# Four batches side by side on the partitions, and a softmax that reduces with transposing VectorE instructions

## Chip, core, metric

One core of a Trainium2 chip. The metric is the device time of one execution in microseconds, the median of several.

## The reference

```python
B, N, D = 8, 4096, 512                       # x and y: float32, 64 MB each
gram = np.matmul(x, y.transpose(0, 2, 1))
diag = np.diagonal(gram, axis1=1, axis2=2)   # only the row-by-row dot products matter
diag = diag - diag.max(axis=-1, keepdims=True)
exp = np.exp(diag)
return exp / exp.sum(axis=-1, keepdims=True) # a softmax over the 4096 rows of each batch
```

## The kernel before

Each batch is spread over all 128 partitions, 32 neighbouring rows (64 KB) on each. There are eight steps of 16 MB. In six of them VectorE multiplies and then sums whole tiles. In the last two it makes one dot product per instruction, and the very last step comes in pieces of 16, 8, 4, 2, 1 and 1 rows, so that little is left to do when the last row lands. A softmax needs the maximum and the sum over all 128 partitions; GpSimd (POOL in the profile) makes both.

```python
xv = x.rearrange("b (p r) d -> b p r d", p=P)         # 64 KB from partition to partition
...                                                   # yv, ov alike; cut
def load_y(b, r0, n):
    nc.sync.dma_start(out=ys[:, r0 : r0 + n, :], in_=yv[b, :, r0 : r0 + n, :])
...                                                   # multiply, sum, dot_row: cut
def group_out(name, b0, n, ssum):                     # batches 0 to 4, then 5 and 6
    ...                                               # reciprocal, scale: cut
    nc.scalar.dma_start(out=ov[:, b0 : b0 + n, :], in_=res[:, b0 : b0 + n, :])

def last_softmax(b):                                  # the tail
    db, rb = diag[:, b, :], res[:, b, :]
    ...
    nc.vector.tensor_reduce(out=mxp, in_=db, axis=X, op=Alu.max)
    nc.gpsimd.partition_all_reduce(out_ap=mx, in_ap=mxp, channels=P, reduce_op=bass_isa.ReduceOp.max)
    nc.vector.tensor_single_scalar(out=nmx, in_=mx, scalar=-1.0, op=Alu.mult)
    nc.scalar.activation(out=rb, in_=db, func=Act.Exp, bias=nmx, scale=1.0, accum_out=sump)
    nc.gpsimd.partition_all_reduce(out_ap=ssum, in_ap=sump, channels=P, reduce_op=bass_isa.ReduceOp.add)
    nc.vector.reciprocal(out=rc, in_=ssum)
    nc.vector.tensor_single_scalar(out=rb, in_=rb, scalar=rc, op=Alu.mult)
    nc.scalar.dma_start(out=ov[:, b, :], in_=rb)
```

Of the kernel before, what the change touches and what calls it, by code (L numbers as in the profile page):

```python
# [1 line left out]

# [5 lines left out]


@with_exitstack
def kernel(
    ctx: ExitStack,
    tc: tile.TileContext,
    x: bass.AP,
    y: bass.AP,
    out: bass.AP,
):
    nc = tc.nc
    ctx.enter_context(tc.manual_schedule())  # L20
    f32 = mybir.dt.float32
    Alu = mybir.AluOpType
    Act = mybir.ActivationFunctionType
    X = mybir.AxisListType.X
    B, N, D = x.shape
    P = nc.NUM_PARTITIONS
    R = N // P
    wide = B - 2


    xv = x.rearrange("b (p r) d -> b p r d", p=P)
    yv = y.rearrange("b (p r) d -> b p r d", p=P)
    ov = out.rearrange("b (p r) -> p b r", p=P)

    big = ctx.enter_context(tc.tile_pool(name="big", bufs=1))
    small = ctx.enter_context(tc.tile_pool(name="small", bufs=1))


    xs = [big.tile([P, R, D], f32, name=f"xs{i}") for i in range(2)]
    ys = big.tile([P, R, D], f32, name="ys")  # L40

    K = 6
    side = big.tile([P, K, D], f32, name="side")
    diag = small.tile([P, B, R], f32, name="diag")
    res = small.tile([P, B, R], f32, name="res")

    def column(name, n):
        return small.tile([P, n], f32, name=name)

    def load_x(b, r0, n):  # L50
        nc.sync.dma_start(out=xs[b % 2][:, r0 : r0 + n, :], in_=xv[b, :, r0 : r0 + n, :])  # L51

    def load_y(b, r0, n):
        nc.sync.dma_start(out=ys[:, r0 : r0 + n, :], in_=yv[b, :, r0 : r0 + n, :])  # L54

    def dots_wide(b, r0, n, yt):
        xt = xs[b % 2][:, r0 : r0 + n, :]
        nc.vector.tensor_tensor(out=xt, in0=xt, in1=yt, op=Alu.mult)  # L58

    def sums_wide(b):  # L60
        nc.vector.tensor_reduce(out=diag[:, b, :], in_=xs[b % 2], axis=X, op=Alu.add)  # L61

    def dot_row(b, r):
        xt = xs[b % 2]
        nc.vector.scalar_tensor_tensor(  # L65
            out=xt[:, r, :],
            in0=xt[:, r, :],
            scalar=1.0,
            in1=ys[:, r, :],
            op0=Alu.mult,  # L70
            op1=Alu.mult,
            accum_out=diag[:, b, r : r + 1],
        )

    def group_exp(name, b0, n):

        mxp, mx, nmx, sump, ssum = (column(name + s, n) for s in ("mxp", "mx", "nmx", "sump", "ssum"))
        nc.vector.tensor_reduce(out=mxp, in_=diag[:, b0 : b0 + n, :], axis=X, op=Alu.max)  # L78
        nc.gpsimd.partition_all_reduce(out_ap=mx, in_ap=mxp, channels=P, reduce_op=bass_isa.ReduceOp.max)  # L79
        nc.scalar.mul(nmx, mx, -1.0)  # L80
        for i in range(n):
            nc.scalar.activation(  # L82
                out=res[:, b0 + i, :], in_=diag[:, b0 + i, :], func=Act.Exp,
                bias=nmx[:, i : i + 1], scale=1.0, accum_out=sump[:, i : i + 1],
            )
        nc.gpsimd.partition_all_reduce(out_ap=ssum, in_ap=sump, channels=P, reduce_op=bass_isa.ReduceOp.add)  # L86
        return ssum

    def group_out(name, b0, n, ssum):
        rc = column(name + "rc", n)  # L90
        nc.vector.reciprocal(out=rc, in_=ssum)  # L91
        for i in range(n):
            rb = res[:, b0 + i, :]
            nc.scalar.activation(out=rb, in_=rb, func=Act.Copy, scale=rc[:, i : i + 1])  # L94
        nc.scalar.dma_start(out=ov[:, b0 : b0 + n, :], in_=res[:, b0 : b0 + n, :])

    def last_softmax(b):
        db, rb = diag[:, b, :], res[:, b, :]
        mxp, mx, nmx, sump, ssum, rc = (column("l" + s, 1) for s in ("mxp", "mx", "nmx", "sump", "ssum", "rc"))
        nc.vector.tensor_reduce(out=mxp, in_=db, axis=X, op=Alu.max)  # L100
        nc.gpsimd.partition_all_reduce(out_ap=mx, in_ap=mxp, channels=P, reduce_op=bass_isa.ReduceOp.max)  # L101
        nc.vector.tensor_single_scalar(out=nmx, in_=mx, scalar=-1.0, op=Alu.mult)  # L102
        nc.scalar.activation(out=rb, in_=db, func=Act.Exp, bias=nmx, scale=1.0, accum_out=sump)  # L103
        nc.gpsimd.partition_all_reduce(out_ap=ssum, in_ap=sump, channels=P, reduce_op=bass_isa.ReduceOp.add)  # L104
        nc.vector.reciprocal(out=rc, in_=ssum)  # L105
        nc.vector.tensor_single_scalar(out=rb, in_=rb, scalar=rc, op=Alu.mult)  # L106
        nc.scalar.dma_start(out=ov[:, b, :], in_=rb)

    for b in range(wide):
        load_x(b, 0, R)  # L110
        load_y(b, 0, R)
        nc.scalar.activation(out=side, in_=ys[:, R - K :, :], func=Act.Copy)  # L112
        dots_wide(b, 0, R - K, ys[:, : R - K, :])
        dots_wide(b, R - K, K, side)
        if b == wide - 1:
            group_out("a", 0, wide - 1, first)
        sums_wide(b)
        if b == wide - 2:
            first = group_exp("a", 0, wide - 1)

    b = B - 2
    load_x(b, 0, R)
    for r0 in (0, R // 2):
        load_y(b, r0, R // 2)
        for r in range(r0, r0 + R // 2):
            dot_row(b, r)

    b = B - 1
    r0 = 0
    for n in (16, 8, 4, 2, 1, 1):  # L130
        load_x(b, r0, n)
        load_y(b, r0, n)
        for r in range(r0, r0 + n):
            if r == 2:
                second = group_exp("b", B - 3, 2)
            if r == 10:
                group_out("b", B - 3, 2, second)
            dot_row(b, r)
        r0 += n
    last_softmax(b)  # L140


# [1 line left out]
_INS = ['x', 'y']  # L144
_OUTS = [((8, 4096), 'float32')]


# [23 lines left out]
```

## Time and profile before

| | before |
|---|---|
| time, median of the first 3 runs | 322.36 us |
| span of the profiled run | 320.3 us |
| loads, first packet to last (packet records) | 1.7 to 314.3 us |
| last landing of y to start of the last dot product | 314.76, 314.85 us |
| start of the last dot product to issue of the last store | 3.08 us |
| issue of the last store to the end | 2.4 us |

The page of the kernel before. The rows of busy tenths have 40 slices of 8 us; "q1" is the load queue and "q10" the store queue, with packets, MB and their share of the 16 DMA engines' time.

```profile
span 320.3 us, 310 instructions
...
DVE 247.8 (77%) x154; ACT 22.7 (7%) x32; POOL 3.3 (1%) x10
...
DMA  9999999999999999999999999999999999999991
GB/s 393 393 393 524 393 393 516 401 393 483 434 393 450 466 393 409 507 393 393 524 393 393 507 409 393 466 450 393 442 475 393 393 456 411 447 419 420 419 411 46
...
q1 hardware_dynamic: 3888, 134.22, 97.3%
q10 hardware_dynamic: 1072, 0.13, 0.3%
...
L58 DVE TENSOR_TENSOR xs<-xs,ys 128x13312 f32<-128x13312 f32 x6 | 84.2, 14025 | 62.6 <-DMA ys<-in_y_dram 62.6
```

The DMA engines are at nine tenths in every slice but the last, and the load queue alone fills 97.3% of them. VectorE (DVE) is busy 77% and waits 62.6 us for y. So this is a kernel at the limit of its loads: nothing that VectorE, ScalarE or POOL saves in mid-stream can shorten it. Time can be gained in two places only: in the load stream itself, and in the tail after the last landing.

The tail, from the timeline (start, duration, engine, line of the kernel and instruction; in brackets how long the engine had been idle, and for whom; ACT is ScalarE, and ACTq its queue, which issues the stores):

```profile
314.85 0.69 DVE L65 SCALAR_TENSOR_TENSOR xs<-xs,ys 128x512 f32<-128x512 f32 x1 [0.57 <-DMA ys<-in_y_dram]
...
315.58 0.19 DVE L100 TENSOR_REDUCE lmxp<-diag 128x1 f32<-128x32 f32 x1
315.87 0.37 POOL L101 PARTITION_ALL_REDUCE lmx<-lmxp  x1 [16.88 <-DVE lmxp L100]
316.26 0.15 DVE L102 TENSOR_SCALAR lnmx<-lmx 128x1 f32<-128x1 f32 x1 [0.49 <-POOL lmx L101]
316.45 0.32 ACT L103 ACTIVATE res<-diag,lnmx 128x32 f32<-128x32 f32 x1 [14.57 <-DVE lnmx L102]
316.68 0.19 ACT L103 ACTIVATION_READ_ACCUMULATOR res<-diag,lnmx 128x1 f32 x1
316.96 0.40 POOL L104 PARTITION_ALL_REDUCE lssum<-lsump  x1 [0.72 <-ACT res L103]
317.39 0.16 DVE L105 RECIPROCAL lrc<-lssum 128x1 f32<-128x1 f32 x1 [0.97 <-POOL lssum L104]
317.66 0.24 DVE L106 TENSOR_SCALAR res<-res,lrc 128x32 f32<-128x32 f32 x1
317.93 0.35 ACTq L107 DMA_DIRECT2D out_dram<-res  x1
```

The two POOL reductions take 0.37 and 0.40 us (spans on POOL are rough in this profile), and each costs hand-overs from VectorE or ScalarE to POOL and back, that is, waits of one engine for the other's signal. The store is issued 3.08 us after the last dot product starts.

Two pieces of the chain of waits (start, duration, what):

```profile
301.92 8.14 DMA out_dram<-res
...
310.12 4.64 DMA ys<-in_y_dram
```

The chain says that the last load of y, issued at 310.12, had waited 8.14 us for the 32 KB store of batches 5 and 6. The two share a completion count (the counter by which the kernel learns that a transfer has landed), so one must end before the other is issued.

### The profile page before, as it was taken

To read this page: it belongs to the slowest core of one execution; us is meant where nothing else is said; L and a number is where in the kernel's file an instruction comes from. 1 tells how busy PE (TensorE), PEld (TensorE's weight loads), DVE (VectorE), ACT (ScalarE), POOL (GpSimd) and SP (SyncE) were. 2 spreads that over 40 slices of the span, in tenths; PEclk is the share of its full clock that TensorE was granted. 3 is DMA by queue.
4 is the path that set the end of the run, shared out by engine and by line. 5 is a ranking of instruction groups with operands and counts; after the bars stand their busy time and mean duration, and the time that the engine had idled before them with its cause. 6 is when DMAs were issued, how large, how long until landed. Compare 5 with 4: busy or idle time off the path is not lost.

```text
span 320.3 us, 310 instructions
## 1 busy us (share of the span) xinstructions
DVE 247.8 (77%) x154; ACT 22.7 (7%) x32; POOL 3.3 (1%) x10
## 2 busy tenths in 40 slices
DVE  0000079995999949999499994999959999993994
ACT  1000030000300002000200003000050100000100
POOL 0000000000000000000000000000000000000100
DMA  9999999999999999999999999999999999999991
GB/s 393 393 393 524 393 393 516 401 393 483 434 393 450 466 393 409 507 393 393 524 393 393 507 409 393 466 450 393 442 475 393 393 456 411 447 419 420 419 411 46
DMA packets 4961, 134.36 MB, mean 419 GB/s; under 512 B 1504, under 2 KB 1504, under 8 KB 2272
## 3 DMA queue, kind: packets, MB, share of 16 engines
q1 hardware_dynamic: 3888, 134.22, 97.3%
q10 hardware_dynamic: 1072, 0.13, 0.3%
q14 instruction: 1, 0.01, 0.0%
HBM read 134.22 MB, written 0.13 MB: 419 GB/s over the span
## 4 chain that ended last, share of the span: by engine, by line
DMA 60%; DVE 36%; issue 2%; SPq 0%; POOLq 0%; ACT 0%; POOL 0%; DVEq 0%; ACTq 0%
DMA ys<-in_y_dram 57%; DVE xs L58 27%; DVE xs L65 5%; DVE diag L61 4%; DMA out_dram<-res 3%; POOLq L166 0%; ACT res L94 0%; SPq L51 0%; POOL lmx L101 0%; DVE res L106 0%; DVE lmxp L100 0%; DVE lrc L105 0%; DVE bmxp L78 0%; SPq L54 0%; DVEq L58 0%
## 5 line engine op out<-in xcount | busy, mean ns | idle before, releaser
L58 DVE TENSOR_TENSOR xs<-xs,ys 128x13312 f32<-128x13312 f32 x6 | 84.2, 14025 | 62.6 <-DMA ys<-in_y_dram 62.6
L61 DVE TENSOR_REDUCE diag<-xs 128x32 f32<-128x16384 f32 x6 | 103.3, 17220 | 0.2
L65 DVE SCALAR_TENSOR_TENSOR xs<-xs,ys 128x512 f32<-128x512 f32 x64 | 39.6, 689 | 5.7 <-DMA ys<-in_y_dram 5.6
L112 ACT ACTIVATE side<-ys 128x3072 f32<-128x3072 f32 x6 | 16.6, 2763 | 185.3 <-DMA ys<-in_y_dram 185.3
L58 DVE TENSOR_TENSOR xs<-xs,side 128x3072 f32<-128x3072 f32 x6 | 20.1, 3352 | 0.0
L65 DVE DVE_READ_ACCUMULATOR xs<-xs,ys 128x1 f32 x64 | 5.4, 84 | 0.0
L80 ACT ACTIVATE bnmx<-bmx 128x2 f32<-128x2 f32 x1 | 0.2, 203 | 42.8 <-POOL bmx L79 42.8
L79 POOL PARTITION_ALL_REDUCE amx<-amxp x1 | 0.4, 386 | 231.5 <-DVE amxp L78 231.5
L80 ACT ACTIVATE anmx<-amx 128x5 f32<-128x5 f32 x1 | 0.2, 208 | 32.7 <-POOL amx L79 32.7
L94 ACT ACTIVATE res<-res,arc 128x32 f32<-128x32 f32 x5 | 1.2, 310 | 14.8 <-DVE arc L91 14.8
L82 ACT ACTIVATE res<-diag,anmx 128x32 f32<-128x32 f32 x5 | 1.5, 309 | 0.0
L79 POOL PARTITION_ALL_REDUCE bmx<-bmxp x1 | 0.7, 736 | 61.7 <-DVE bmxp L78 61.7
L103 ACT ACTIVATE res<-diag,lnmx 128x32 f32<-128x32 f32 x1 | 0.3, 321 | 14.6 <-DVE lnmx L102 14.6
L112 ACT ACT_TABLE_LOAD x1 | 1.3, 1283 | 0.7 <-PEq L155 0.7
L82 ACT ACTIVATION_READ_ACCUMULATOR res<-diag,anmx 128x1 f32 x5 | 0.9, 188 | 0.0
L105 DVE RECIPROCAL lrc<-lssum 128x1 f32<-128x1 f32 x1 | 0.2, 164 | 1.0 <-POOL lssum L104 1.0
L86 POOL PARTITION_ALL_REDUCE bssum<-bsump x1 | 0.8, 797 | 1.1 <-ACT res L82 1.1
L94 ACT ACTIVATE res<-res,brc 128x32 f32<-128x32 f32 x2 | 0.5, 312 | 3.2 <-DVE brc L91 3.2
L82 ACT ACTIVATE res<-diag,bnmx 128x32 f32<-128x32 f32 x2 | 0.6, 314 | 0.0
L101 POOL PARTITION_ALL_REDUCE lmx<-lmxp x1 | 0.4, 367 | 16.9 <-DVE lmxp L100 16.9
L102 DVE TENSOR_SCALAR lnmx<-lmx 128x1 f32<-128x1 f32 x1 | 0.2, 153 | 0.5 <-POOL lmx L101 0.5
L86 POOL PARTITION_ALL_REDUCE assum<-asump x1 | 0.5, 459 | 2.0 <-ACT res L82 2.0
(13 smaller groups left out, 2.7 us busy)
## 6 DMA issues: line engine op xcount, KB each, us to landing
ys<-in_y_dram SPq DMA_DIRECT2D x3, 4096.0 KB, 15.0
xs<-in_x_dram SPq DMA_DIRECT2D x1, 4096.0 KB, 14.7
xs<-in_x_dram SPq DMA_DIRECT2D x1, 2048.0 KB, 19.2
ys<-in_y_dram SPq DMA_DIRECT2D x1, 2048.0 KB, 19.6
xs<-in_x_dram SPq DMA_DIRECT2D x1, 1024.0 KB, 8.0
ys<-in_y_dram SPq DMA_DIRECT2D x1, 1024.0 KB, 10.2
xs<-in_x_dram SPq DMA_DIRECT2D x1, 512.0 KB, 11.0
ys<-in_y_dram SPq DMA_DIRECT2D x1, 512.0 KB, 11.7
```

The costliest lines, as they stand in the source:

```text
L58: nc.vector.tensor_tensor(out=xt, in0=xt, in1=yt, op=Alu.mult)
L61: nc.vector.tensor_reduce(out=diag[:, b, :], in_=xs[b % 2], axis=X, op=Alu.add)
L65: nc.vector.scalar_tensor_tensor(out=xt[:, r, :], in0=xt[:, r, :], scalar=1.0, in1=ys[:, r, :], op0=Alu.mult, op1=Alu.mult, accum_out=diag ...
L79: nc.gpsimd.partition_all_reduce(out_ap=mx, in_ap=mxp, channels=P, reduce_op=bass_isa.ReduceOp.max)
L80: nc.scalar.mul(nmx, mx, -1.0)
L82: nc.scalar.activation(out=res[:, b0 + i, :], in_=diag[:, b0 + i, :], func=Act.Exp, bias=nmx[:, i : i + 1], scale=1.0, accum_out=sump[:, i ...
L86: nc.gpsimd.partition_all_reduce(out_ap=ssum, in_ap=sump, channels=P, reduce_op=bass_isa.ReduceOp.add)
L94: nc.scalar.activation(out=rb, in_=rb, func=Act.Copy, scale=rc[:, i : i + 1])
L101: nc.gpsimd.partition_all_reduce(out_ap=mx, in_ap=mxp, channels=P, reduce_op=bass_isa.ReduceOp.max)
L102: nc.vector.tensor_single_scalar(out=nmx, in_=mx, scalar=-1.0, op=Alu.mult)
L103: nc.scalar.activation(out=rb, in_=db, func=Act.Exp, bias=nmx, scale=1.0, accum_out=sump)
L112: nc.scalar.activation(out=side, in_=ys[:, R - K :, :], func=Act.Copy)
```

## The change

The intent: four batches lie side by side, each on 32 partitions, with 128 rows (256 KB) per partition. A maximum or a sum then has to cross only 32 partitions, which a VectorE reduction that transposes 32x32 blocks can do, without POOL. The Trainium skill, "VectorE: DVE Perf Modes", section "The three transpose paths", describes VectorE's transpose as a grid of independently transposed 32x32 blocks, hence one batch per 32 partitions. Batches 0 to 3 take four steps and batches 4 to 7 four more. The steps move the same bytes in the same pieces as before, but neighbouring partitions now read addresses 256 KB apart instead of 64 KB. The maximum over the early columns is taken before the last rows land, and the stores become 256 packets of 512 B instead of 1024 of 128 B.

```diff
-    xv = x.rearrange("b (p r) d -> b p r d", p=P)
-    yv = y.rearrange("b (p r) d -> b p r d", p=P)
-    ov = out.rearrange("b (p r) -> p b r", p=P)
+    xv = x.rearrange("(s b) (j c) d -> s (b j) c d", b=Q, j=G)      # Q = 4, G = 32
+    yv = y.rearrange("(s b) (j c) d -> s (b j) c d", b=Q, j=G)
+    ov = out.rearrange("(s b) (j c) -> s (b j) c", b=Q, j=G)
 ...                                                # loads and products: same sizes, cut
+    def over_quadrant(name, column, op, negate=False):
+        got = small.tile([P, 1], f32, name=name)
+        nc.vector.tensor_reduce(
+            out=got, in_=column.to_broadcast([P, G]), axis=X, op=op, negate=negate, apply_transpose=True
+        )
+        return got
 ...                                                # group_exp, group_out, last_softmax go
+    def exps(i, d):
+        mxp = small.tile([P, 1], f32, name=f"mxp{i}")
+        largest(mxp, d)
+        nmx = over_quadrant(f"nmx{i}", mxp, Alu.max, negate=True)
+        sump = small.tile([P, 1], f32, name=f"sump{i}")
+        nc.scalar.activation(out=res[i], in_=diag[i][:, :C], func=Act.Exp, bias=nmx, scale=1.0, accum_out=sump)
+        return sump
+    def store(i, sump, n):
+        total = over_quadrant(f"sum{i}", sump, Alu.add)
+        rc = small.tile([P, 1], f32, name=f"rc{i}")
+        nc.vector.reciprocal(out=rc, in_=total)
+        nc.vector.tensor_single_scalar(out=res[i], in_=res[i], scalar=rc, op=Alu.mult)
+        for p in range(0, P, n):
+            nc.scalar.dma_start(out=ov[i, p : p + n, :], in_=res[i][p : p + n, :])
 ...                                                # steps 0 to 6: cut
     for n in (16, 8, 4, 2, 1, 1):
         load_x(t, r0, n)
         load_y(t, r0, n)
+        if r0 == 0:
+            largest(diag[1][:, C : C + 1], diag[1][:, : C - R])
+        if r0 == R - 2:
+            largest(diag[1][:, C + 1 :], diag[1][:, C - R : C - 2])
         dots(t, r0, n)
         r0 += n
+    store(1, exps(1, diag[1][:, C - 2 :]), P)
```

More of the change, by code (lines that the diff above doesn't have):

```diff
@@ L26 @@
     P = nc.NUM_PARTITIONS
-    R = N // P
-    wide = B - 2
-    xv = x.rearrange("b (p r) d -> b p r d", p=P)
-    yv = y.rearrange("b (p r) d -> b p r d", p=P)
-    ov = out.rearrange("b (p r) -> p b r", p=P)
+    G = 32
+    Q = P // G
+    C = N // G
+    R = 32
+    H = R // 2
+    K = 6
+    S = B // Q * (C // R)
+    xv = x.rearrange("(s b) (j c) d -> s (b j) c d", b=Q, j=G)
+    yv = y.rearrange("(s b) (j c) d -> s (b j) c d", b=Q, j=G)
+    ov = out.rearrange("(s b) (j c) -> s (b j) c", b=Q, j=G)
     big = ctx.enter_context(tc.tile_pool(name="big", bufs=1))
@@ L40 @@
     ys = big.tile([P, R, D], f32, name="ys")
-    K = 6
     side = big.tile([P, K, D], f32, name="side")
-    diag = small.tile([P, B, R], f32, name="diag")
-    res = small.tile([P, B, R], f32, name="res")
-    def column(name, n):
-        return small.tile([P, n], f32, name=name)
-    def load_x(b, r0, n):
-        nc.sync.dma_start(out=xs[b % 2][:, r0 : r0 + n, :], in_=xv[b, :, r0 : r0 + n, :])
-    def load_y(b, r0, n):
-        nc.sync.dma_start(out=ys[:, r0 : r0 + n, :], in_=yv[b, :, r0 : r0 + n, :])
@@ L56, in dots_wide @@
-    def dots_wide(b, r0, n, yt):
-        xt = xs[b % 2][:, r0 : r0 + n, :]
-        nc.vector.tensor_tensor(out=xt, in0=xt, in1=yt, op=Alu.mult)
-    def sums_wide(b):
-        nc.vector.tensor_reduce(out=diag[:, b, :], in_=xs[b % 2], axis=X, op=Alu.add)
-    def dot_row(b, r):
-        xt = xs[b % 2]
-        nc.vector.scalar_tensor_tensor(
-            out=xt[:, r, :],
-            in0=xt[:, r, :],
-            scalar=1.0,
-            in1=ys[:, r, :],
-            op0=Alu.mult,
-            op1=Alu.mult,
-            accum_out=diag[:, b, r : r + 1],
-        )
@@ L75, in group_exp @@
-    def group_exp(name, b0, n):
-        mxp, mx, nmx, sump, ssum = (column(name + s, n) for s in ("mxp", "mx", "nmx", "sump", "ssum"))
-        nc.vector.tensor_reduce(out=mxp, in_=diag[:, b0 : b0 + n, :], axis=X, op=Alu.max)
-        nc.gpsimd.partition_all_reduce(out_ap=mx, in_ap=mxp, channels=P, reduce_op=bass_isa.ReduceOp.max)
-        nc.scalar.mul(nmx, mx, -1.0)
-        for i in range(n):
-            nc.scalar.activation(
-                out=res[:, b0 + i, :], in_=diag[:, b0 + i, :], func=Act.Exp,
-                bias=nmx[:, i : i + 1], scale=1.0, accum_out=sump[:, i : i + 1],
-            )
-        nc.gpsimd.partition_all_reduce(out_ap=ssum, in_ap=sump, channels=P, reduce_op=bass_isa.ReduceOp.add)
-        return ssum
@@ L89, in group_out @@
-    def group_out(name, b0, n, ssum):
-        rc = column(name + "rc", n)
-        nc.vector.reciprocal(out=rc, in_=ssum)
-        for i in range(n):
-            rb = res[:, b0 + i, :]
-            nc.scalar.activation(out=rb, in_=rb, func=Act.Copy, scale=rc[:, i : i + 1])
-        nc.scalar.dma_start(out=ov[:, b0 : b0 + n, :], in_=res[:, b0 : b0 + n, :])
-    def last_softmax(b):
-        db, rb = diag[:, b, :], res[:, b, :]
-        mxp, mx, nmx, sump, ssum, rc = (column("l" + s, 1) for s in ("mxp", "mx", "nmx", "sump", "ssum", "rc"))
-        nc.vector.tensor_reduce(out=mxp, in_=db, axis=X, op=Alu.max)
-        nc.gpsimd.partition_all_reduce(out_ap=mx, in_ap=mxp, channels=P, reduce_op=bass_isa.ReduceOp.max)
-        nc.vector.tensor_single_scalar(out=nmx, in_=mx, scalar=-1.0, op=Alu.mult)
-        nc.scalar.activation(out=rb, in_=db, func=Act.Exp, bias=nmx, scale=1.0, accum_out=sump)
-        nc.gpsimd.partition_all_reduce(out_ap=ssum, in_ap=sump, channels=P, reduce_op=bass_isa.ReduceOp.add)
-        nc.vector.reciprocal(out=rc, in_=ssum)
-        nc.vector.tensor_single_scalar(out=rb, in_=rb, scalar=rc, op=Alu.mult)
-        nc.scalar.dma_start(out=ov[:, b, :], in_=rb)
@@ L109 @@
-    for b in range(wide):
-        load_x(b, 0, R)
-        load_y(b, 0, R)
-        nc.scalar.activation(out=side, in_=ys[:, R - K :, :], func=Act.Copy)
-        dots_wide(b, 0, R - K, ys[:, : R - K, :])
-        dots_wide(b, R - K, K, side)
-        if b == wide - 1:
-            group_out("a", 0, wide - 1, first)
-        sums_wide(b)
-        if b == wide - 2:
-            first = group_exp("a", 0, wide - 1)
-    b = B - 2
-    load_x(b, 0, R)
-    for r0 in (0, R // 2):
-        load_y(b, r0, R // 2)
-        for r in range(r0, r0 + R // 2):
-            dot_row(b, r)
@@ L128, with columns, rows, dots_of @@
-    b = B - 1
+    diag = [small.tile([P, C + 2 * i], f32, name=f"diag{i}") for i in range(B // Q)]
+    res = [small.tile([P, C], f32, name=f"res{i}") for i in range(B // Q)]
+    def columns(t, r0, n):
+        c0 = t % (C // R) * R + r0
+        return slice(c0, c0 + n)
+    def rows(t, r0, n):
+        return xs[t % 2][:, r0 : r0 + n, :]
+    def dots_of(t, r0, n):
+        return diag[t * R // C][:, columns(t, r0, n)]
+    def load_x(t, r0, n):
+        nc.sync.dma_start(out=rows(t, r0, n), in_=xv[t * R // C, :, columns(t, r0, n), :])
@@ new lines, in load_y, with products, sums, dots @@
+    def load_y(t, r0, n):
+        nc.sync.dma_start(out=ys[:, r0 : r0 + n, :], in_=yv[t * R // C, :, columns(t, r0, n), :])
+    def products(t, r0, n, yt):
+        xt = rows(t, r0, n)
+        nc.vector.tensor_tensor(out=xt, in0=xt, in1=yt, op=Alu.mult)
+    def sums(t, r0, n):
+        nc.vector.tensor_reduce(out=dots_of(t, r0, n), in_=rows(t, r0, n), axis=X, op=Alu.add)
+    def dots(t, r0, n):
+        for r in range(r0, r0 + n):
+            xt = xs[t % 2][:, r, :]
+            nc.vector.scalar_tensor_tensor(
+                out=xt, in0=xt, scalar=1.0, in1=ys[:, r, :], op0=Alu.mult, op1=Alu.mult,
+                accum_out=dots_of(t, r, 1),
+            )
@@ new lines, in over_quadrant, with largest @@
+    def over_quadrant(name, column, op, negate=False):
+        got = small.tile([P, 1], f32, name=name)
+        nc.vector.tensor_reduce(
+            out=got, in_=column.to_broadcast([P, G]), axis=X, op=op, negate=negate, apply_transpose=True
+        )
+        return got
+    def largest(out, d):
+        nc.vector.tensor_reduce(out=out, in_=d, axis=X, op=Alu.max)
+    def exps(i, d):
[5 more added lines that the diff above has]
+        return sump
@@ new lines, in store @@
+    def store(i, sump, n):
[5 more added lines that the diff above has]
+            nc.scalar.dma_start(out=ov[i, p : p + n, :], in_=res[i][p : p + n, :])
+    for t in range(S - 2):
+        load_x(t, 0, R)
+        load_y(t, 0, R)
+        nc.scalar.activation(out=side, in_=ys[:, R - K :, :], func=Act.Copy)
+        products(t, 0, R - K, ys[:, : R - K, :])
+        if t == C // R:
+            store(0, sump, G)
+        products(t, R - K, K, side)
+        sums(t, 0, R)
+        if t == C // R - 1:
+            sump = exps(0, diag[0])
@@ L129 @@
+    t = S - 2
+    load_x(t, 0, R)
+    for r0 in (0, H):
+        load_y(t, r0, H)
+        dots(t, r0, H)
+    t += 1
     r0 = 0
     for n in (16, 8, 4, 2, 1, 1):
-        load_x(b, r0, n)
-        load_y(b, r0, n)
-        for r in range(r0, r0 + n):
-            if r == 2:
-                second = group_exp("b", B - 3, 2)
-            if r == 10:
-                group_out("b", B - 3, 2, second)
-            dot_row(b, r)
+        load_x(t, r0, n)
+        load_y(t, r0, n)
+        if r0 == 0:
+            largest(diag[1][:, C : C + 1], diag[1][:, : C - R])
+        if r0 == R - 2:
+            largest(diag[1][:, C + 1 :], diag[1][:, C - R : C - 2])
+        dots(t, r0, n)
@@ L139 @@
         r0 += n
-    last_softmax(b)
+    store(1, exps(1, diag[1][:, C - 2 :]), P)
 _INS = ['x', 'y']
```

## The prediction

> **What bounds the kernel now.** The loads. The page gives 134.22 MB read in a span of 320.3 us, the load queue holds 97.3% of the 16 DMA engines' time, VectorE is busy 77%. In the packet records the loads run without a gap from 1.7 us to about 314.3 us (434 GB/s in the steady part; the median 64 KB packet takes 2418 ns). The 62.6 us in which VectorE waits for y are this same limit. The span is about 1.7 us of start, 312.6 us of loads, and 6 us of tail.
>
> **What the change does.**
> 1. The loads keep their bytes, count, order and sizes; each partition still reads 64 KB in a row. Only the pitch between partitions grows from 64 KB to 256 KB. The Trainium skill, "DMA: Bandwidth & Descriptors", section "Latency and other measured facts", reports copies of 16 KiB rows at 207 GB/s with a 512 KiB pitch, 164 at 2 MiB, and calls 214 full. So 256 KB lies at the harmless end; my estimate is 0 to 1% of 312 us (0 to 3 us), most likely nothing. No trace here shows it yet. It is the one term that can be large: all of it is on the critical path.
> 2. Stores: 1024 packets of 128 B become 256 of 512 B; in mid-stream 896 become 128. Their queue holds 0.3% of the engines' time. Estimate: 0.4 to 0.9 us less in the load stream.
> 3. Mid-stream softmax: about 1 us of VectorE work in place of POOL and a chain of small ScalarE operations. VectorE has slack, and x buffers come free 4 us before the queue runs dry (x issued at 231.5, the y ahead of it lands at 235.6): worth nothing. The wait of the last y load on the 32 KB store (8.14 us in the chain of waits) goes, but the packet rate shows the engines full until 312.5, so it buys 0 to 0.5 us.
> 4. Tail after the last landing (314.76). Now: dot 0.71, max 0.20, POOL 0.37, negate 0.15, exp 0.32+0.19, POOL 0.40, reciprocal 0.16, scale 0.24 and hand-overs: the output is issued at 317.93, 3.1 us after the dot starts. After: a maximum over 4 columns instead of 32 (estimate 0.15), two transposing reductions of 128x32 (about 0.2 each) replace both POOL calls and the negation, exp and scale over 128 columns cost about 0.1 more each: 2.5 us, so 0.5 to 0.6 us saved. The last store is 64 KB instead of 16 KB in the same 128 packets: +0.1 us.
>
> **Sum.** 322.4 - 0.6 (stores) - 0.5 (tail) + 0 to 3 (pitch): about 321.5 us, the same within 2%. Range 320.4 to 325.5 us. Chances: faster by over 2% 1%; within 2% 89%; slower by over 2% 10%.
>
> **What the profile would show.**
> - Step 1: 64 KB packets stay near a median of 2418 ns, steady slices near 434 GB/s. If pitch costs, this median grows, the DMA row stays full, the GB/s row falls, and VectorE's waits on y lengthen.
> - Step 2: the store queue falls to about 0.1%.
> - Step 3: DMA stays at nine tenths in all slices but the last; POOL has only its four memsets.
> - Step 4: from the last row product's start to the last store's issue about 2.5 us.
>
> **What would make it wrong.** A conflict of the 16 engines' streams in HBM, now farther apart, would slow all loads: 5% gives 337 us. The small last loads (2 KB per partition) could suffer more, but are a few MB. A dearer transposing reduction, or stores split in four that hold back a load through a shared completion count, would cost at most a few us.

## The result and the profile after

The changed kernel is correct. It took 321.45 us (321.21 to 321.74, 6 runs) against 322.13 us before (321.80 to 322.72, 6 runs): ratio 0.9977, 95% interval 0.9965 to 0.9990. All ratios here are the mean time of one kernel's runs over that of the other's of the same rounds, so they are not quite the ratios of the quoted medians.

The change was then run twice more: 322.13 us (ratio 0.9993) and 321.83 us (0.9991). Over its 17 runs the changed kernel averages 321.75 us (321.21 to 322.64); the 44 runs of the kernel before average 322.17 us (321.80 to 322.87). So the gain is about 0.4 us, and the first set flattered it.

The page of the changed kernel:

```profile
span 319.5 us, 284 instructions
...
DVE 249.1 (78%) x158; ACT 18.9 (6%) x11; POOL 0.2 (0%) x4
...
DMA  9999999999999999999999999999999999999992
GB/s 394 394 394 517 402 394 484 435 394 468 435 410 394 492 427 394 484 435 394 435 476 402 394 509 410 394 492 429 396 414 484 390 419 447 415 431 410 424 411 101
...
q1 hardware_dynamic: 3888, 134.22, 97.6%
q10 hardware_dynamic: 336, 0.13, 0.1%
...
L69 DVE TENSOR_TENSOR xs<-xs,ys 128x13312 f32<-128x13312 f32 x6 | 84.2, 14025 | 62.3 <-DMA ys<-in_y_dram 62.3
```

The DMA row has not changed, the steady slices still swing about the same level (a slice counts a packet whole, hence the swing), and VectorE waits 62.3 us for y instead of 62.6. POOL is down to its four start-up memsets. The packet records give the same median as before for a 64 KB packet, 2418 ns. The store queue fell from 0.3% to 0.1%, and the loads lasted 312.3 us instead of 312.6. The load queue's share rose from 97.3% to 97.6%, but the span is shorter, and over all runs with 64 KB packets this share scatters from 97.2% to 97.7%.

The tail of the changed kernel, from the timeline:

```profile
314.62 0.69 DVE L77 SCALAR_TENSOR_TENSOR xs<-xs,ys 128x512 f32<-128x512 f32 x1 [0.46 <-DMA ys<-in_y_dram]
...
315.35 0.16 DVE L91 TENSOR_REDUCE mxp<-diag 128x1 f32<-128x4 f32 x1
315.54 0.21 DVE L85 TRANSPOSE_TENSOR_REDUCE nmx<-mxp 128x1 f32<-128x32 f32 x1
315.79 0.40 ACT L98 ACTIVATE res<-diag,nmx 128x128 f32<-128x128 f32 x1 [76.83 <-DVE nmx L85]
316.10 0.19 ACT L98 ACTIVATION_READ_ACCUMULATOR res<-diag,nmx 128x1 f32 x1
316.32 0.21 DVE L85 TRANSPOSE_TENSOR_REDUCE sum<-sump 128x1 f32<-128x32 f32 x1 [0.56 <-ACT res L98]
316.56 0.16 DVE L104 RECIPROCAL rc<-sum 128x1 f32<-128x1 f32 x1
316.76 0.29 DVE L105 TENSOR_SCALAR res<-res,rc 128x128 f32<-128x128 f32 x1
317.08 0.36 ACTq L107 DMA_DIRECT2D out_dram<-res  x1
```

From the last dot product to the store it is now 2.46 us, 0.62 us less. The maximum, the negation and the crossing of the partitions took from 315.58 to 316.45 (0.87 us) before; now they take from 315.35 to 315.79 (0.44 us). From the exponential to the reciprocal it was 0.94 us and is 0.77 us, although the exponential reads 128 columns instead of 32.

The chain of waits, at the place where before had the store and the held load (one line):

```profile
304.44 10.09 DMA ys<-in_y_dram
```

The store is gone from the chain and the last load of y goes out 5.7 us earlier, yet it lands at 314.53 instead of 314.76. The queue was full; it only waited in another place.

### The profile page after: what moved, and what is told of

It is laid out like the page before. It is cut to its first block, busy times and chain, and to the rows that moved or that the text cites. A ratio compares the mean times of both kernels' runs of the same rounds, so it can differ in the third digit from the quotient of the medians.

```text
span 319.5 us, 284 instructions
## 1 busy us (share of the span) xinstructions
DVE 249.1 (78%) x158; ACT 18.9 (6%) x11; POOL 0.2 (0%) x4
## 3 DMA queue, kind: packets, MB, share of 16 engines
q1 hardware_dynamic: 3888, 134.22, 97.6%
## 4 chain that ended last, share of the span: by engine, by line
DMA 60%; DVE 36%; issue 2%; SPq 0%; ACT 0%; DVEq 0%
DMA ys<-in_y_dram 60%; DVE xs L69 27%; DVE xs L77 5%; DVE diag L72 4%; SPq L62 0%; DVE res L105 0%; DVE sum L85 0%; DVE nmx L85 0%; ACT res L98 0%; DVE rc L104 0%; DVE mxp L91 0%; SPq L65 0%; DVEq L69 0%; DVEq L77 0%
## 5 line engine op out<-in xcount | busy, mean ns | idle before, releaser
L69 DVE TENSOR_TENSOR xs<-xs,ys 128x13312 f32<-128x13312 f32 x6 | 84.2, 14025 | 62.3 <-DMA ys<-in_y_dram 62.3
L98 ACT ACTIVATE res<-diag,nmx 128x128 f32<-128x128 f32 x2 | 0.8, 402 | 109.2 <-DVE nmx L85 109.2
```

The lines of the kernel that those rows point to most:

```text
L69: nc.vector.tensor_tensor(out=xt, in0=xt, in1=yt, op=Alu.mult)
L98: nc.scalar.activation(out=res[i], in_=diag[i][:, :C], func=Act.Exp, bias=nmx, scale=1.0, accum_out=sump)
```

## Experiments

Three accounts compete. **Tail**: the whole gain is the 0.62 us in the tail, and the rest does nothing. **Stream**: thinner stores and the freed last load shorten the load stream. **Pitch**: the wider pitch costs something, which the stores hide. "Wrong" means that the values differ from the reference by construction.

The first four runs were made on one chip, with 11 runs of the kernel before.

**The changed kernel again**, no edit.

> The changed kernel unedited, as the yardstick for the three runs beside it. Expected: ratio to before 0.9977 give or take 0.0013, that is 321.2 to 321.8 us; from the start of the last row product to the issue of the last store 2.46 us again (before: 3.08 us). If that 0.62 us is a property of the code and not of one profile, it repeats within 0.05 us.

Measured: 322.13 us (321.23 to 322.64), ratio 0.9993 (0.9979 to 1.0007). The tail repeated to the hundredth, 2.46 us. The total did not: the expected ratio was missed. In the profiled execution the loads ended at 315.1 us instead of 314.1.

**The old addresses** (wrong): the changed kernel, reading with the old pitch.

```diff
-    xv = x.rearrange("(s b) (j c) d -> s (b j) c d", b=Q, j=G)
+    xv = x.rearrange("b (p r) d -> b p r d", p=P)          # y alike; loads index [t, :, r0 : r0 + n, :]
```

> The changed kernel with the old addresses of the loads (64 KB pitch, one batch per step; wrong values on purpose, same instructions, same bytes). My theory (the pitch is free): ratio to the changed kernel 1.000 within 0.0015, so about 321.4 us, median of the 64 KB packets 2418 ns, loads last 312.3 us. Rival (the pitch costs a little and hides a part of the gain of the thinner stores): this kernel is 0.3 to 1 us faster than the changed one, 320.4 to 321.1 us, and its loads last under 312.0 us.

Measured: 321.33 us (321.05 to 321.83), ratio to before 0.9974 (0.9963 to 0.9986); packet median 2418 ns, loads 312.5 us in the profiled run. Beside the repeat of the changed kernel this is 0.8 us better in the median, as the pitch account wants; beside the first set of the changed kernel it is nothing, and its loads are not under 312.0 us. Inconclusive alone.

**A pitch of 512 KB** (wrong).

```diff
-    xv = x.rearrange("(s b) (j c) d -> s (b j) c d", b=Q, j=G)
+    xv = x.rearrange("b (j s r) d -> s (b j) r d", s=S, r=R)   # y alike
```

> The changed kernel with 512 KB between partitions, the widest pitch that 128 partitions of these inputs allow (wrong values on purpose). My theory (64 KB in a row per partition hide the pitch): the same as the changed kernel within 0.2%, 321.4 us, packet median 2418 ns. Rival (the copies of 16 KiB rows in the Trainium skill carry over: 207 of 214 GB/s at 512 KiB): loads 3.4% longer, 312 to 323 us, whole kernel about 332 us.

Measured: 321.78 us (321.53 to 322.04), ratio 0.9985 (0.9974 to 0.9997), packet median 2418 ns. Doubling the pitch again costs nothing that can be told from the scatter of the changed kernel's own sets, and the loss of 3.4% is excluded. That the figure for copies carries over is refuted for these loads.

**POOL back in the tail** (wrong in the last four batches).

```diff
-        nmx = over_quadrant(f"nmx{i}", mxp, Alu.max, negate=True)
+        mx = over_all("mx", mxp, bass_isa.ReduceOp.max)       # partition_all_reduce; for i == 1 alone
+        nc.vector.tensor_single_scalar(out=nmx, in_=mx, scalar=-1.0, op=Alu.mult)
 ...
-        total = over_quadrant(f"sum{i}", sump, Alu.add)
+        total = over_all("sum1", sump, bass_isa.ReduceOp.add) # for i == 1 alone
```

> The changed kernel with the two transposing reductions of its last softmax put back to POOL reductions over all partitions and a negation on VectorE (wrong values in the last four batches on purpose). My theory (0.6 us of the 0.7 us gain is this tail): from the start of the last product to the issue of the last store about 3.1 us instead of 2.46 us, total 322.0 us, 0.6 us over the changed kernel. Rival (the gain is in the load stream, by thinner stores and a freed last load): stays within 0.2 us of the changed kernel.

Measured: 322.64 us (321.69 to 322.86), ratio to before 1.0006 (0.9994 to 1.0018). The gain is gone; beside the repeat of the changed kernel in the same rounds it is 0.5 us more in the median. The timeline of this run:

```profile
315.53 0.69 DVE L77 SCALAR_TENSOR_TENSOR xs<-xs,ys 128x512 f32<-128x512 f32 x1 [0.39 <-DMA ys<-in_y_dram]
...
316.26 0.16 DVE L96 TENSOR_REDUCE mxp<-diag 128x1 f32<-128x4 f32 x1
316.52 0.35 POOL L92 PARTITION_ALL_REDUCE mx<-mxp  x1 [316.09 <-DVE mxp L96]
316.90 0.15 DVE L106 TENSOR_SCALAR nmx<-mx 128x1 f32<-128x1 f32 x1 [0.48 <-POOL mx L92]
317.09 0.40 ACT L108 ACTIVATE res<-diag,nmx 128x128 f32<-128x128 f32 x1 [77.92 <-DVE nmx L106]
...
317.67 0.38 POOL L92 PARTITION_ALL_REDUCE sum<-sump  x1 [0.81 <-ACT res L108]
318.09 0.16 DVE L114 RECIPROCAL rc<-sum 128x1 f32<-128x1 f32 x1 [1.03 <-POOL sum L92]
...
318.68 0.36 ACTq L117 DMA_DIRECT2D out_dram<-res  x1
```

And three pieces of its chain of waits ("issue" is time for which the profile shows no cause, "POOLq" is POOL's own queue):

```profile
316.52 0.35 POOL mx L92
316.87 0.76 issue
317.62 0.44 POOLq L174
```

The dot product starts at 315.53 and the store is issued at 318.68: 3.15 us. The chain can't tell the price of the hand-overs, because the exponential and its read-out run within its 0.76 us of "issue". The timeline can. Against the changed kernel, the path from the maximum to the exponential takes 0.83 us instead of 0.44, from there to the reciprocal 1.00 instead of 0.77, and from there to the store 0.59 instead of 0.52. Of these 0.69 us, 0.46 are longer instructions (0.35 + 0.38 us on POOL and 0.15 for the negation, against two times 0.21); the other 0.23 lie between instructions, in hand-overs.

The next four runs shared a chip and 11 runs of the kernel before.

**The kernel before without its mid-stream stores** (wrong: seven batches unwritten).

```diff
-        nc.scalar.dma_start(out=ov[:, b0 : b0 + n, :], in_=res[:, b0 : b0 + n, :])
```

> The kernel before without its two mid-stream stores (896 packets of 128 B; seven batches are left unwritten on purpose). It bounds from above what thinner stores and the freed last load of y can give. My theory after the result: the loads last 0.3 to 0.6 us less than the 312.6 us of before, total 321.5 to 321.9 us. Rival (stores interleave for nothing): within 0.15 us of before. The prediction's 0.4 to 0.9 us would give 321.2 to 321.7 us.

Measured: 322.13 us (321.81 to 322.69), ratio 1.0004 (0.9992 to 1.0016). My expectation failed and so did the prediction's term. Its queues, from the page:

```profile
q1 hardware_dynamic: 3888, 134.22, 97.3%
q10 hardware_dynamic: 144, 0.02, 0.0%
```

The stores' 0.3% went to 0.0%, the load queue kept its 97.3% of a span of 320.9 us, and the execution was not shorter. Removing all 896 packets gives nothing that these runs resolve (the interval allows 0.26 us at most), so making fewer of them cannot give 0.4.

**Transposing reductions in the kernel before** (wrong in the last batch, because each quadrant of 32 partitions is normalized alone).

```diff
-        nc.gpsimd.partition_all_reduce(out_ap=mx, in_ap=mxp, channels=P, reduce_op=bass_isa.ReduceOp.max)
-        nc.vector.tensor_single_scalar(out=nmx, in_=mx, scalar=-1.0, op=Alu.mult)
+        nc.vector.tensor_reduce(
+            out=nmx, in_=mxp.to_broadcast([P, 32]), axis=X, op=Alu.max, negate=True, apply_transpose=True
+        )
 ...                                                          # the sum likewise
```

> The kernel before with the POOL reductions and the negation of its last softmax replaced by two transposing reductions on VectorE (wrong values in the last batch on purpose: each quadrant is normalized alone). My theory: product to store issue falls from 3.08 us to about 2.4 us, total down by 0.6 to 0.7 us, about 321.5 us, so this alone gives nearly the whole gain of the change. Rival (the gain comes with the layout and the stores): under 0.2 us of gain.

Measured: 321.42 us (321.14 to 322.03), ratio 0.9979 (0.9967 to 0.9991). Lines of its timeline:

```profile
314.90 0.69 DVE L65 SCALAR_TENSOR_TENSOR xs<-xs,ys 128x512 f32<-128x512 f32 x1 [0.57 <-DMA ys<-in_y_dram]
...
315.63 0.19 DVE L100 TENSOR_REDUCE lmxp<-diag 128x1 f32<-128x32 f32 x1
315.86 0.21 DVE L101 TRANSPOSE_TENSOR_REDUCE lnmx<-lmxp 128x1 f32<-128x32 f32 x1
316.10 0.32 ACT L104 ACTIVATE res<-diag,lnmx 128x32 f32<-128x32 f32 x1 [14.12 <-DVE lnmx L101]
...
316.55 0.21 DVE L105 TRANSPOSE_TENSOR_REDUCE lssum<-lsump 128x1 f32<-128x32 f32 x1 [0.48 <-ACT res L104]
...
317.27 0.35 ACTq L110 DMA_DIRECT2D out_dram<-res  x1
```

The store is issued 2.37 us after the dot product starts, as expected. The two reductions alone, in the old layout with the old pitch and the old stores, give the gain of the first set of the whole change.

**The last load of y freed from the store** (right values): the last two one-row loads of x made one, which moves the last y to another completion count.

```diff
-        load_x(b, r0, n)
+        if r0 < R - 1:
+            load_x(b, r0, 2 if r0 == R - 2 else n)
         load_y(b, r0, n)
```

> The kernel before with the last two one-row loads of x made one two-row load, so that the last load of y no longer waits for the 32 KB store (right values). My theory (the engines are full anyway): last landing of y at 314.5 to 314.8 us instead of 314.76 us, total within 0.3 us of before. Rival (the held load cost time): last landing before 314.3 us, total 0.4 us or more under before.

Measured: 322.16 us (321.91 to 322.48), ratio 1.0000 (0.9988 to 1.0012). The chain of waits at the place where the store stood:

```profile
301.27 12.76 DMA ys<-in_y_dram
...
314.13 1.32 DVE xs L65 x4
```

The store is gone from the chain. The very last y landed at 314.67, against 314.76 in before, although it was issued before 305 and not at 310.12. The row before the last landed later, at 314.04, because two rows of x were now ahead of it, so two dot products follow. The hold of 8.14 us in the chain was no cost that these runs resolve (the interval is 0.4 us to either side).

**Mid-stream store of the changed kernel in 512 packets of 128 B** (right values).

```diff
-        for p in range(0, P, n):
-            nc.scalar.dma_start(out=ov[i, p : p + n, :], in_=res[i][p : p + n, :])
+        for c in range(0, C, 32):                              # for i == 0 alone
+            nc.scalar.dma_start(out=ov[i, :, c : c + 32], in_=res[i][:, c : c + 32])
```

> The changed kernel with its mid-stream store in pieces of 32 columns: 512 packets of 128 B instead of 128 of 512 B, as many DMAs (right values). Theory (a store packet costs its time on an engine, about 13 ns, and a bit for the switch): 384 more packets over 16 engines add 0.3 to 0.5 us, total 321.7 to 321.9 us. Rival (small stores are free in the shadow of the loads): within 0.15 us of the changed kernel.

Measured: 321.55 us (321.16 to 321.80), ratio 0.9979 (0.9967 to 0.9991). Four times as many store packets in mid-stream cost nothing visible; the rival of that expectation holds beside the first set of the changed kernel (321.45 us), which did not run in the same rounds. This kernel reads at 256 KB pitch and is as fast as the one at 64 KB.

The next three were made on one chip with 7 runs of the kernel before. **All loads cut into pieces of 4 KB per partition**, at three pitches (64 and 512 KB wrong).

```diff
+        for r1 in range(r0, r0 + n, 2):
+            load_x2(t, r1, min(2, n))                           # y alike
```

> All loads of the changed kernel cut into pieces of two rows (4 KB per partition, 512 KB each), at 64 KB pitch (wrong values on purpose). The yardstick for the next run: 4 KB packets take 159 to 160 ns in the traces of before and after, so 32768 of them over 16 engines need about 326 us; total 335 to 345 us.

> The same pieces of 4 KB at 256 KB pitch (right values). Theory (pitch is free because each partition reads a long run in a row): with 4 KB runs the engines now jump 256 KB every 160 ns, and the pitch should begin to show, 1 to 5% over the run at 64 KB pitch. Rival (pitch up to 256 KB never matters on a single core): within 0.3% of the run at 64 KB pitch, packet mean within 1 ns.

> The same pieces of 4 KB at 512 KB pitch (wrong values on purpose). If runs of 4 KB expose the pitch: 3% or more over the run at 64 KB pitch, as in the copies that the Trainium skill reports. Rival: within 0.3% of it.

Measured: 341.82 us at 64 KB (ratio 1.0611), 341.08 at 256 KB (1.0590), 341.39 at 512 KB (1.0603). The median packet takes 161 ns at all three pitches. The 64 KB run lies in the range expected for it. My theory that short runs would expose the pitch failed. What costs 6% is the cutting itself, smaller packets and smaller DMAs (512 KB at most) together. The rates of the 64 KB and of the 256 KB run, from their pages:

```profile
GB/s 279 415 409 409 410 411 409 409 409 409 409 410 410 409 409 410 409 410 410 410 409 409 409 410 410 410 252 413 411 409 409 409 408 410 411 410 409 408 407 108
```

```profile
GB/s 308 412 409 410 410 409 410 409 409 409 410 410 409 410 409 410 409 409 409 409 410 410 409 411 409 410 279 413 410 407 410 409 410 410 410 410 410 409 405 77
```

The steady slices stand at 409 to 410 GB/s at either pitch, where 64 KB packets ran at 434 GB/s in the packet records. The one low slice near 225 us (252 and 279) falls together with the mid-stream store: in the waits of the 256 KB run one load of x waits 5.0 us for a store that shares its completion count. The DMA row falls from 9 to 7 in that slice, so here the engines did run dry. That the shortness of the queued loads is the reason is likely, but no run isolates it.

**The changed kernel a third time**, no edit, with 9 runs of before.

> The changed kernel unedited once more, because its first two sets differ (0.9977 and 0.9993) and the run at 64 KB pitch beside the second lay at 0.9974. If the end of the load stream merely scatters from execution to execution: a ratio between 0.997 and 0.9995, product to store issue 2.46 us, and a last landing anywhere from 314.5 to 315.6 us. If the second set was the true level and the 64 KB pitch really is 0.8 us better: a ratio of 0.999 or more. If the first was: 0.9977 within 0.0007.

Measured: 321.83 us (321.57 to 321.91), ratio 0.9991 (0.9977 to 1.0004); tail 2.46 us, last landing 314.90. The ratio lies where two of the three expectations overlap, so this run alone did not decide.

What scatters can be read from the trace: each load ends with 16 completion signals, which I take to be one from each of the 16 engines. For the last load of y they came at these times (us from the start of the span):

| profiled run | first signal | median | last signal | span |
|---|---|---|---|---|
| before | 313.48 | 313.67 | 314.76 | 320.3 |
| change, first set | 313.39 | 313.75 | 314.53 | 319.5 |
| change, second set | 313.38 | 314.10 | 315.60 | 320.5 |
| change, third set | 313.30 | 313.85 | 314.90 | 319.8 |
| old addresses | 313.59 | 313.81 | 314.63 | 319.6 |
| before, no mid-stream stores | 313.20 | 313.75 | 315.15 | 320.9 |

The first signal lies within 0.4 us in all of them. The last one moves by 1.1 us, in one and the same kernel too, and the span follows it. Why one signal lags, and by how much, no run here explains.

What the span has beyond the last signal is the tail, free of that scatter. Unrounded, it is 4.92 to 4.93 us in all six profiles with the tail of the change and 64 KB packets, at 64, 256 and 512 KB pitch and with thin or small stores. It is 4.86 us for the transposing reductions in the old layout, and 5.58 to 5.75 us in all four profiles with POOL in the tail (before, POOL back, no mid-stream stores, last y freed). The times agree: the 38 runs of the first kind, the old layout included, average 321.63 us, the 59 of the second 322.20 us. That is 0.57 us less, near the 0.62 us of the tail.

## Why the prediction was right

- **Total** (321.5 us, range 320.4 to 325.5): right. The first set gave 321.45 us, the 17 runs average 321.75 us. The nearness of the first figure is partly luck: one term of the sum was not there, the terms without a pitch cost add up to 321.3 us, and the first set lies 0.3 us under the average of all.
- **What bounds it**: right. Loads fill the DMA engines before and after, and no change to the stores or to the held load showed in the time.
- **Step 1, pitch 0 to 1%, most likely nothing**: right. The packet median stayed at 2418 ns at 64, 256 and 512 KB; with 4 KB packets it is 161 ns at all three. A difference of a few tenths of a us between 64 and 256 KB is not excluded: two sets of the changed kernel lie higher than the run at the old addresses, the first set and the variant with small store packets hardly do. Pooled over the kernels with transposing tails, 11 runs at 64 KB average 321.45 us, 22 at 256 KB 321.69 us. With 4 KB packets the order is reversed (341.82 and 341.08 us; the intervals overlap).
- **Step 2, stores, "0.4 to 0.9 us less in the load stream"**: this is the term that was mis-sized. The packets fell as predicted and their share went to 0.1%, but the stream did not shorten: without any mid-stream store the kernel before took 1.0004 of its time, and with 384 store packets more the changed kernel kept its 0.9979. I took the time of packets on an average engine off the stream. The span follows the last of the 16 completion signals, and that one scatters by more than the term. Nor do the load queue's shares show a trade: it has 97.6% beside the old stores (transposing reductions in the kernel before) and 97.2% beside the thin ones (POOL back in the tail).
- **Step 3, mid-stream softmax and freed last load, "0 to 0.5 us"**: right, at its low end as far as the runs resolve: freed alone, 1.0000 (0.9988 to 1.0012). The mid-stream softmax has no run of its own; VectorE's waits for y stayed the same (62.6 and 62.3 us).
- **Step 4, tail 2.5 instead of 3.1 us**: right: 2.46 instead of 3.08 us, in all three profiles, with transposing reductions of 0.21 us each. The reductions give 0.69 us in the new layout (3.15 to 2.46) and 0.71 in the old (3.08 to 2.37); the wider exponential and scaling give back 0.07 to 0.09 net of the smaller maximum. The larger last store lands 1.6 us after its issue instead of 1.4, but from its issue to the end it is 2.4 us in both. This part is shown from both sides: the reductions put into the old kernel bring 0.9979, POOL put back into the new one takes the gain away (1.0006).

So the sum that holds is 322.17 - 0.62 = 321.55 us. The observed mean is 321.75; the 0.2 us between them are within what the last signal scatters, a small cost of the pitch would fit them too, and they stay open.

## What to carry to other kernels

In a kernel that keeps the DMA engines full from start to end, price a change by the tail after the last landing, and count a saving in the stream only if the last completion signal comes earlier, not if the average DMA engine has less to do. A wait in the chain behind a full queue need not be a cost: ask whether the engines would have moved anything else meanwhile. When a gain is a few tenths of a per cent, repeat the unedited kernel before you explain it; here the tail repeated to 0.01 us while the total moved by 0.2%.

## What the Trainium skill lacked or had wrong

- "VectorE: DVE Perf Modes", section "Why `tensor_reduce` can't reduce along partition axis", and "GPSIMD Engine Reference", section "When to use GPSIMD", which calls GpSimd the only option for a cross-partition reduce: here a VectorE reduction with a built-in transpose reduced a column over each 32 partitions in 0.21 us, with right results, and the tail was 0.62 us shorter than with POOL.
- The same GpSimd page gives no figure for a partition all-reduce of one column: 0.35 to 0.40 us of POOL time in these tails. With the hand-overs and a negation, two of them make the path from dot product to store 0.7 us longer than two transposing reductions do in the same layout (3.15 against 2.46 us, 3.08 against 2.37 us).
- "DMA: Bandwidth & Descriptors", section "Latency and other measured facts", lists pitch losses for copies between HBM tensors from 512 KiB up. It has no figure for loads into SBUF: here 512 KB pitch cost nothing measurable, with 64 KB packets (ratio 0.9985 to before) or 4 KB packets (1.0603 against 1.0611 at 64 KB).
- The same page asks for 512 B or more per transfer for line rate (section "Specifications") and 1 MiB or more per DMA for the highest bandwidth (section "Rules for kernel authors"). It does not compare 4 KB with 64 KB per partition in one full stream. Here there is still a step: 409 to 410 against 434 GB/s, 161 ns for a 4 KB packet where a sixteenth of the 64 KB packet's 2418 ns is 151 ns. The cut DMAs were 512 KB, under the 1 MiB of the page, and no run separates the two.
- No page gives a figure for how far apart the 16 completion signals of one load come: 1.0 to 2.2 us between the first and the last for the last load of y in the runs above, different from run to run of the same kernel.
